# Retention values as seven block products in one stage, retention as one run of 32 chunks, rotation beside the queries' and keys' products

## The chip, the cores and the metric

The kernel runs on one core of a Trainium2 chip. The metric is the device time of one execution in microseconds, as the median of several runs; lower is better. The engines of the core work side by side, each through its own list of instructions in order: TensorE (PE, with its weight loads shown as PEld), VectorE (DVE), ScalarE (ACT), GpSimd (POOL) and SyncE (SP), which here only starts DMA transfers. POOL starts transfers too, through a queue of its own, among them those that add what they carry to what lies at their destination.

## The reference

One decoder block on a sequence of 1024 tokens of width 1024. Its input is normalised and modulated to `h`; `h @ w_in` gives everything that the two mixers need. The part that the change concerns is retention, with 4 heads, keys of 256, values of 512 and chunks of 128 tokens:

```
rq = rotary(heads(rq, RET_HEADS), pos)
rk = rotary(heads(rk, RET_HEADS), pos) * (RET_DK ** -0.5)
ro = retention(rq, rk, heads(rv, RET_HEADS))
...
    def step(state, inp):
        qi, ki, vi = inp
        s = jnp.einsum('bhid,bhjd->bhij', qi, ki) * inner_decay[None]
        o = (jnp.einsum('bhij,bhje->bhie', s, vi)
             + jnp.einsum('bhid,bhde->bhie', qi, state) * q_decay[None, :, :, None])
        state = (state * chunk_decay[None, :, None, None]
                 + jnp.einsum('bhjd,bhje->bhde', ki * k_decay[None, :, :, None], vi))
        return state, o
...
ro = group_norm(ro) * gn_g + gn_b
ret_out = (jax.nn.silu(rg) * ro) @ w_ret_out
```

`rv` is a product of 1024 tokens by 1024 inputs by 2048 columns (512 a head), `rg` the same size. Beside this stand twelve heads of dilated attention, two gates, the output projections and an MLP.

## The kernel before

Every product is done in float32 by three passes: each operand is split into a high part, which PE takes at full rate, and a low part, the rest; `mm3` (line 195) multiplies low by high, high by low and high by high into one PSUM bank. A split is a copy on ACT (high) and a subtraction on DVE (low).

The steps run in this order: input norm and the attention's values (`av_first`, `av_step`); the queries' and keys' stage (`queries_keys`, line 976); then for each of four heads the retention values (`v_first`, `v_rest`) and eight chunks (`chunk`); then attention, projections and MLP. `Steps` holds the list of steps with their weight loads: loads go out on SP's queue into a ring of three tiles (`wraw`, tag `raw`), `prepare` splits them, and a step's body may call `ahead(n)` to have the next step's loads prepared at that point of its own work. `first["release"]` lets the loads of the next group of steps start.

The queries' and keys' stage multiplies in blocks. `h` and the weights are cut into 2 x 2 blocks, and the product of a pair of 128-column tiles is done by seven block products in place of eight (`Blocks`, line 213; `ORDER` names the seven: 11, s1, s3, s2, 12, 22, s4). The sums of blocks of `h` (`t1` to `t4`) are formed once by `sums_of_h`; `t4` takes the place of the second halves of the even tiles `hh`, `hl`, which are saved to memory before (`h12_d`) and brought back at the end of the stage by eight POOL transfers (lines 994 and 995). `BA.run` goes through 18 pairs (`PAIRS`) times seven products; after each it calls `post`, which turns finished banks into outputs, and `before` and `after`, in which loads and the end of the stage are placed by hand. A pair is of retention (`r`), attention (`a`) or gates (`g`), and the string in `PAIRS` gives their order. Outputs and temporaries are tiles of `xpool` (`x4`, a ring of 26). At the start of this stage `weight_sums` has POOL form the seven blocks of the output projection's weights in memory, by `dma_sum`: one transfer writes, a second adds, and each waits for the one whose result it takes.

The retention values are plain products: per head `v_first` does the first half of the depth for the first four chunks, `v_rest` the rest, 8 chunks x 8 depth tiles x 3 matmuls. Between them lie the previous head's last transposition (`on_T`) and its gating (`u_final`: two ACT passes that scale and shift, a DVE multiply by the Silu of `rg`, a write-out to `y_d`), and in `v_rest` the rotation of the head's queries and keys, six DVE operations on 1024 columns for each of the two (`rotate`).

A chunk does on PE, in this order: the new state's terms (`kv`), a half of its share of the gate product `rg`, the next chunk's scores and key transposition (`s_kt`), the chunk's output (`o`, from the state's high and low part and from the scores), the transposition of the previous chunk's normalised output (`on_T`), the rest of `rg`. On DVE: the state's update (line 737), weight preparation (`ahead`), the scores' decay and split, the state's low part, statistics and normalisation (lines 760 to 766). PSUM outside `rg` is a ring of four banks in this part, so `o` takes the bank of the first `kv`.

Of the kernel before, what the change touches and what calls it, by code (L numbers as in the profile page):

```python
# [17 lines left out]
P = 128  # L18
# [116 lines left out]
def block_kernel(ctx, tc, io, stop=None, dbg=None):  # L135
# [191 lines left out]
    xpool = x_ctx.enter_context(tc.tile_pool(name="xpool", bufs=1))  # L327
# [203 lines left out]
    ws_d = {n: dram.tile([P, 4, 1024], F32, name=f"wro{n}") for n in ("11", "12", "22", "s1", "s2", "s3", "s4")}  # L531
# [7 lines left out]
    def weight_sums(t):  # L539

        for i, v in enumerate((VC_GNG, VC_GNB)):
            nc.vector.tensor_copy(gnv[i][:, :16], vec[:, v:v + 16])
            nc.vector.tensor_scalar_mul(gnv[i][:, 16:], vec[:, v:v + 16], -1.0)
        nc.gpsimd.tensor_tensor(pad[:, NK:NK + 1], fv(t)[:, :1], mhalf[:, :1], op=ALU.mult)
        b11, b12, b21, b22 = (io["w_ret_out"][i] for i in range(4))
        dma_sum(ws_d["s1"], b21, b22)
        dma_sum(ws_d["s3"], b21, b11)
        dma_sum(ws_d["s2"], ws_d["s1"], b11)
        dma_sum(ws_d["s4"], ws_d["s2"], b12)
        for n, b in (("11", b11), ("12", b12), ("22", b22)):  # L550
            nc.gpsimd.dma_start(ws_d[n], b)
# [8 lines left out]
    hd = {}  # L560

    def new_head(h):
        hd["qk"] = R["p"].tile([P, 4, S], F32, tag="qk", name=f"qk{h}")
        for i in range(4):
            nc.sync.dma_start(hd["qk"][:, i, :], qk_d[h][i])

    def rotate(h, i):

        x1, x2 = hd["qk"][:, 2 * i, :], hd["qk"][:, 2 * i + 1, :]
        cos, sin = cs[:, 0, :], cs[:, 1, :]  # L570
        t1, t2 = etile(f"t1_{h}{i}"), etile(f"t2_{h}{i}")
        nc.vector.tensor_mul(t2, x2, sin)
        yield
        nc.vector.tensor_mul(t1, x1, sin)
        yield
        nc.vector.tensor_mul(x1, x1, cos)
        yield
        nc.vector.tensor_mul(x2, x2, cos)
        yield
        nc.vector.tensor_sub(x1, x1, t2)  # L580
        yield
        nc.vector.tensor_add(x2, x2, t1)
        yield

    qk_d = [[dram.tile([P, S], F32, name=f"qkd{h}{i}") for i in range(4)] for h in range(H)]
# [4 lines left out]
    def wv_prep(raw):  # L590
        hi, lo = etile(raw.name + "vh", F32R), etile(raw.name + "vl", F32R)
        nc.scalar.copy(hi, raw)
        nc.vector.tensor_sub(lo, raw, fv(hi))
        return hi, lo

    def jit_qk(h, c):
        p = R["p"]
        src = hd["qk"][:, :, c * C:(c + 1) * C]
        t = p.tile([P, 2, 4, C], F32R, tag="j", bufs=2, name=f"j{h}{c}")
        nc.scalar.copy(t[:, 0], src)  # L600
        nc.gpsimd.tensor_sub(t[:, 1], src, fv(t[:, 0]))  # L601
        hd["j", c] = t

    def s_kt(h, c):

        p = R["p"]
        t = hd["j", c]
# [7 lines left out]
        if pk is not None:  # L615
            for i in range(2):
                nc.tensor.transpose(pk[:, i, :], hd["qk"][:, 2 + i, c * C:(c + 1) * C], ident)
# [8 lines left out]
        hd["s", c] = (smh, sml)  # L626
        if pk is not None:
# [5 lines left out]
            hd["k", c] = (kh, kl)  # L633

    def v_mm(ps, wv, c, ks=range(NK)):

        tok = slice(c * C, (c + 1) * C)
        for k in ks:
            w = wv[k // 2]
            ws = slice((k % 2) * 512, (k % 2) * 512 + 512)  # L640
            nc.tensor.matmul(ps, hl[k][:, tok], w[0][:, ws], start=k == 0, stop=False)  # L641
            nc.tensor.matmul(ps, hh[k][:, tok], w[1][:, ws], start=False, stop=False)  # L642
            nc.tensor.matmul(ps, hh[k][:, tok], w[0][:, ws], start=False, stop=k == NK - 1)  # L643

    def v_first(h):

        def body(ahead, *ws):
            hd["wv"] = list(ws)
            mms = [ps_mm(f"v{h}{i}") for i in range(2)]
            pss = hd["vp"] = [mms[c // 2][:, c % 2, :] for c in range(4)]  # L650
            for c in range(4):
                v_mm(pss[c], ws, c, range(4))
                if c == 1 and h > 0:
                    on_T(h - 1, NC - 1)
                    u_final(h - 1, (0, 1))
                    ahead(0)
                    u_final(h - 1, (2, 3))
            ahead(0)
        return body

    def v_rest(h):
        def body(ahead, *ws):
            p = R["p"]
            ws = hd["wv"] + list(ws)
            vh, vl = [], []
            for c in range(0, NC, 2):
                for lst, n in ((vh, "vh"), (vl, "vl")):
                    t = vtile(f"{n}{h}{c}", F32R)
                    lst += [t[:, :DV], t[:, DV:]]
            hd["v"] = list(zip(vh, vl))  # L670
            rot = itertools.chain(rotate(h, 0), rotate(h, 1))
            for n, c in enumerate((0, 2, 1, 3, 4, 5, 6, 7)):
                if c < 4:
# [1679 lines left out]
```

## Time and profile before

| | |
|---|---|
| median of 3 runs | 2267.89 us (2263.89 to 2268.91) |
| the profiled execution's own time | 2273.85 us |
| its span in the profile | 2272.1 us |
| PE busy | 2207.8 us, 97% |
| DVE busy | 1430.8 us, 63% |
| ACT busy | 884.5 us, 39% |
| POOL busy | 119.6 us, 5% |
| DMA | 345.97 MB, mean 152 GB/s |
| mean granted clock of PE | 0.995 |

In the profile, Lnn is a line of the kernel; `out<-in` names tiles without their numbers; an `x` and a number count instructions; the figure in brackets behind a row is the engine's idle time just before it and what ended that. Windows are stretches of the span, in us from its start. A matmul row's duration runs to its modelled end, so rows overlap.

### The profile page before, as it was taken

How to read it: one execution, taken by the hardware profiler on the slowest of the kernel's cores; microseconds unless marked ns; L12 is line 12 of the kernel's file. 1: busy time of each engine (PE TensorE's matmuls, PEld its weight loads, DVE VectorE, ACT ScalarE, POOL GpSimd, SP SyncE). 2: the span in 40 equal slices, each digit the busy share in tenths (PEclk: the TensorE clock that was granted, in tenths of full speed). 3: DMA queues.
4: the chain of work that ended last, by engine and by line, in shares of the span. 5: the costliest groups of instructions: out<-in, count | busy, mean ns of one | idle time of the engine just before them, and what ended most of it. 6: DMA issues, size and time to landing. Idle time of an engine off the chain costs nothing.

```text
span 2272.1 us, 26840 instructions
## 1 busy us (share of the span) xinstructions
PE 2207.8 (97%) x10226; PEld 1822.8 (80%) x10226; DVE 1430.8 (63%) x2201; ACT 884.5 (39%) x1629; POOL 119.6 (5%) x132
## 2 busy tenths in 40 slices
PE   7999999999999999999999999999999999999998
PEld 5887878888878787888878788888777777788887
DVE  6525565546768776764555554576866665787845
ACT  4323233222434333344534633434454444433412
POOL 0000000001102010100000000002100000000003
PEclk9999999999999999999999999999999999999999
DMA  9549933334322323239822345645134443654322
GB/s 357 198 145 259 308 122 109 111 110 148 121 93 84 131 73 139 75 106 268 234 84 89 108 176 205 242 161 175 63 140 146 153 153 138 246 172 167 121 84 75
DMA packets 125903, 345.97 MB, mean 152 GB/s; under 512 B 24358, under 2 KB 35885, under 8 KB 123054
## 3 DMA queue, kind: packets, MB, share of 16 engines
q1 hardware_dynamic: 121726, 302.31, 38.2%
q0 software_dynamic: 4048, 41.94, 6.9%
q8 instruction: 80, 1.31, 0.2%
q14 instruction: 49, 0.40, 0.1%
HBM read 270.13 MB, written 116.28 MB: 170 GB/s over the span
## 4 chain that ended last, share of the span: by engine, by line
PE 73%; DVE 11%; DMA 8%; ACT 5%; issue 2%; SPq 0%; POOL 0%; DVEq 0%; POOLq 0%; ACTq 0%
PE av L799 4%; PE qap L201 3%; PE qap L205 3%; PE qap L203 3%; PE rg L201 3%; PE rg L203 3%; PE rg L205 3%; PE fp L201 2%; PE fp L203 2%; PE fp L205 2%; PE v L641 2%; PE v L643 2%; PE v L642 2%; PE f2a L203 2%; PE f2a L205 2%
## 5 line engine op out<-in xcount | busy, mean ns | idle before, releaser
L201 PE MATMUL qap<-hh,qaw 128*128 128x512 f32 x216 | 85.2, 395 | 6.8 <-ACT qat L280 4.8
L203 PE MATMUL qap<-hl,qaw 128*128 128x512 f32 x216 | 84.5, 391 | 0.0
L205 PE MATMUL qap<-hh,qaw 128*128 128x512 f32 x216 | 84.5, 391 | 0.0
L258 DVE TENSOR_TENSOR qaw<-wa,qaw 128x512 fp32r<-128x512 f32 x54 | 36.6, 690 | 50.9 <-ACT qaw L248 50.5
L1817 ACT ACTIVATE a<-a 128x512 f32<-128x512 f32 x48 | 30.3, 632 | 84.8 <-DVE a L1816 84.8
L601 POOL TENSOR_TENSOR j<-qk,j 128x512 fp32r<-128x512 f32 x32 | 43.9, 1370 | 366.0 <-ACT j L600 366.0
L1170 ACT ACTIVATE P<-P,ng 128x128 f32<-128x128 f32 (+1 forms) x96 | 41.9, 438 | 39.2 <-DVE ng L1167 39.2
L258 DVE TENSOR_TENSOR fw<-w1r,fw 128x512 fp32r<-128x512 f32 x48 | 33.0, 688 | 37.5 <-ACT fw L248 37.5
L201 PEld LDWEIGHTS qap<-hh,qaw 128*128 128x128 f32 x216 | 40.9, 189 | 16.9 <-ACT qat L280 5.6
L2001 ACT CAST w2h<-w2s 128x512 fp32r<-128x512 f32 x36 | 22.4, 621 | 79.9 <-DVE w2s L2039 79.9
L679 ACT CAST vh<-v 128x512 fp32r<-128x512 f32 x32 | 18.8, 587 | 88.1 <-PE v L643 86.0
L621 ACT COPY sm<-sT 128x128 f32<-128x128 f32 x32 | 8.5, 266 | 114.1 <-PE sT L612 114.1
L248 ACT CAST qaw<-wa 128x512 fp32r<-128x512 f32 x54 | 32.4, 617 | 46.8 <-PE qap L205 28.0
L201 PE MATMUL fp<-h2h,fw 128*128 128x512 f32 x128 | 50.0, 390 | 0.0
L203 PE MATMUL fp<-h2l,fw 128*128 128x512 f32 x128 | 49.8, 389 | 0.0
L201 PE MATMUL roa<-rh,rwl 128*128 128x512 f32 x128 | 49.8, 389 | 0.0
L203 PE MATMUL roa<-rl,rwh 128*128 128x512 f32 x128 | 49.8, 389 | 0.0
L205 PE MATMUL roa<-rh,rwh 128*128 128x512 f32 x128 | 49.8, 389 | 0.0
L205 PE MATMUL fp<-h2h,fw 128*128 128x512 f32 x128 | 49.8, 389 | 0.0
L1714 POOL TENSOR_TENSOR accnf<-accnf,sqnf 128x256 f32<-128x256 f32 (+1 forms) x18 | 16.6, 921 | 628.1 <-ACT sqnf L1713 628.1
L1551 DVE TENSOR_TENSOR rwl<-rwl,rwh 128x1024 fp32r<-128x1024 f32 x25 | 30.2, 1221 | 29.0 <-ACT rwh L1582 29.0
L203 PEld LDWEIGHTS qap<-hl,qaw 128*128 128x128 f32 x216 | 41.0, 190 | 8.5
(3161 smaller groups left out, 7162.2 us busy)
## 6 DMA issues: line engine op xcount, KB each, us to landing
raw<-in_w_ada_dram SPq DMA_DIRECT2D x32, 512.0 KB, 3.5
w1r<-in_w_ff_dram SPq DMA_DIRECT2D x32, 512.0 KB, 4.9
yt<-y POOLq DMA_DIRECT2D x6, 2048.0 KB, 16.2
xsd<-as SPq DMA_DIRECT2D x24, 512.0 KB, 2.7
w2r<-in_w_ff2s_dram SPq DMA_DIRECT2D x24, 512.0 KB, 7.2
em<-in_w_ada_dram SPq DMA_DIRECT2D x16, 512.0 KB, 10.2
wros<-in_w_ret_out_dram POOLq DMA_DIRECT2D x4, 2048.0 KB, 16.4
qkd<-qa SPq DMA_DIRECT2D x16, 512.0 KB, 3.0
```

The lines of the kernel that those rows point to most:

```text
L201: nc.tensor.matmul(o, wl, xh, start=first, stop=False, skip_group_check=skip)
L203: nc.tensor.matmul(o, wh, xl, start=False, stop=False, skip_group_check=skip)
L205: nc.tensor.matmul(o, wh, xh, start=False, stop=last, skip_group_check=skip)
L248: nc.scalar.copy(t[:, :512], src)
L258: nc.vector.tensor_sub(t[:, 512:], src, fv(t[:, :512]))
L601: nc.gpsimd.tensor_sub(t[:, 1], src, fv(t[:, 0]))
L641: nc.tensor.matmul(ps, hl[k][:, tok], w[0][:, ws], start=k == 0, stop=False)
L642: nc.tensor.matmul(ps, hh[k][:, tok], w[1][:, ws], start=False, stop=False)
L643: nc.tensor.matmul(ps, hh[k][:, tok], w[0][:, ws], start=False, stop=k == NK - 1)
L799: nc.tensor.matmul(av[g][c], x[k][:, c * C:(c + 1) * C], w[j][:, ws], start=k == 0 and (x, j) == parts[0], stop=k == NK - 1 and (x, j) == ...
L1170: nc.scalar.activation(v, v, AF.Exp, bias=ng[:, blk:blk + 1], accum_out=st[:, g, blk, 2 + a:3 + a])
L1817: nc.scalar.activation(o, o, AF.Relu)
```

## The change

The values are formed for all heads in one stage behind the queries' and keys' products, by seven block products for each of two halves of the columns: 14 items (`VSEQ`), each four token tiles. The weights' blocks come from memory, summed by POOL at the start of the queries' and keys' stage, ahead of the output projection's. The items take the sums of `h` as the stationary operand; results leave already split, as high and low part, for `v_d`. The restores of `hh` and `hl` and the release of the next loads move behind the first token tile of the last item. `fetch` then brings, three chunks ahead, a chunk's rotated queries and keys (256 KB) and its values (512 KB).

The rotation is taken into the queries' and keys' stage: after each product one DVE operation on 512 columns for the retention pair before, 12 a pair, and then the write-out to `qk_d`. `PAIRS` is reordered so that retention pairs are spread out. `xpool` gets the option `reuse_waits="tile"`, which the other pools of the later stages have already.

The 32 chunks follow each other without a values' stage between them. The gating of a head is done one tile at a time at the end of the first four chunks of the next. In the first chunk of all, its whole share of `rg` goes ahead of `kv`. `u_final`, `on_T`, `s_kt` and `jit_qk` keep their instructions, indexed by a running number. The code leaves out `v_first`, `v_rest`, `new_head`, `wv_prep`, `vtile` and the old `rotate`.

```diff
-    xpool = x_ctx.enter_context(tc.tile_pool(name="xpool", bufs=1))
+    xpool = x_ctx.enter_context(tc.tile_pool(name="xpool", bufs=1, reuse_waits="tile"))
...
-        return R["p"].tile([P, 1024], dt, tag="E", bufs=8, name=name)
-
-    def vtile(name, dt=F32):
-        return R["p"].tile([P, 1024], dt, tag="V", bufs=8, name=name)
+        return R["p"].tile([P, 1024], dt, tag="E", bufs=12, name=name)
...
+        for dst, src in ((wv_d, io["w_rv"]), (ws_d, io["w_ret_out"])):
+            b11, b12, b21, b22 = (src[i] for i in range(4))
+            dma_sum(dst["s1"], b21, b22)
+            dma_sum(dst["s3"], b21, b11)
+            dma_sum(dst["s2"], dst["s1"], b11)
+            dma_sum(dst["s4"], dst["s2"], b12)
+            for n, b in (("11", b11), ("12", b12), ("22", b22)):
+                nc.gpsimd.dma_start(dst[n], b)
...
+    def fetch(i):
+
+        h, c = divmod(i, NC)
+        if i > 1:
+            hd["qk", i] = R["p"].tile([P, 4, C], F32, tag="qk", bufs=4, name=f"qk{h}{c}")
+        elif i == 0:
+            t = whl.tile([P, 1024], F32, tag="wl", name="qk01").rearrange("p (a b c) -> p a b c", a=2, b=4)
+            for j in range(2):
+                hd["qk", j] = t[:, j]
+                nc.sync.dma_start(t[:, j], qk_d[0][:, :, j * C:(j + 1) * C])
+        if i > 1:
+            nc.sync.dma_start(hd["qk", i], qk_d[h][:, :, c * C:(c + 1) * C])
+        if i > 0:
+            v = R["p"].tile([P, 2, DV], F32R, tag="V", bufs=4, name=f"v{h}{c}")
+        else:
+            v = whl.tile([P, 1024], F32R, tag="wh", name="v00").rearrange("p (a b) -> p a b", a=2)
+        hd["v", i] = v
+        nc.sync.dma_start(fv(v), v_d[h][:, c])
...
     def chunk(h, c, ahead, w=None):
         p = R["p"]
-        if c == 0:
-            hd["srg"] = [etile(f"srg{h}{e}") for e in range(4)]
+        g = NC * h + c
+        if g + 3 < NG:
+            fetch(g + 3)
         if c % 2 == 0:
             hd["rgw"] = w
             hd["rgp"] = ps_mm(f"rg{h}{c}")
-        if c == 6 and h + 1 < H:
-            new_head(h + 1)
         ks = range(4 * (c % 2), 4 * (c % 2) + 4)
-        vh, vl = hd["v"][c]
+        if g == 0:
+            proj_mm(hd["rgp"], hd["rgw"], ks)
...
-            on_T(h, c - 1)
-        proj_mm(hd["rgp"], hd["rgw"], ks[2:])
+        if g + 2 < NG:
+            jit_qk(g + 2)
+        if g > 0:
+            on_T(*divmod(g - 1, NC))
+        if g > 0:
+            proj_mm(hd["rgp"], hd["rgw"], ks[2:])
...
-        hd["o", c] = on
+        hd["o", h, c] = on
         if c % 2 == 1:
-            nc.scalar.activation(hd["srg"][c // 2], flat(hd["rgp"]), AF.Silu)
-
-    def head_tail(h):
-        on_T(h, NC - 1)
-        u_final(h)
+            hd["srg", h, c // 2] = etile(f"srg{h}{c // 2}")
+            nc.scalar.activation(hd["srg", h, c // 2], flat(hd["rgp"]), AF.Silu)
+        if h > 0 and c < 4:
+            u_final(h - 1, (c,))
...
-    PAIRS = [{"r": r_pairs, "a": a_pairs, "g": g_pairs}[i].pop(0) for i in "ragragragragrrarar"]
+    PAIRS = [{"r": r_pairs, "a": a_pairs, "g": g_pairs}[i].pop(0) for i in "rargrargrargrargaa"]
...
+    def rotate(q):
+
+        _, t, h = PAIRS[q]
+        u, v = BA.t[q]
+        for hf in range(2):
+            hs = slice(512 * hf, 512 * hf + 512)
+            x1, x2, cos, sin = OA[q][0][:, hs], OA[q][1][:, hs], cs[:, 0, hs], cs[:, 1, hs]
+            for f, o, x, y in ((nc.vector.tensor_mul, u, x2, sin), (nc.vector.tensor_mul, v, x1, sin),
+                               (nc.vector.tensor_mul, x1, x1, cos), (nc.vector.tensor_mul, x2, x2, cos),
+                               (nc.vector.tensor_sub, x1, x1, u), (nc.vector.tensor_add, x2, x2, v)):
+                f(o, x, y)
+                yield
+        for i in range(2):
+            nc.sync.dma_start(qk_d[h][:, 2 * (t == "k") + i], OA[q][i])
...
+        turns = []
         def after(q, n):
-            if q == NA - 1 and n == "s2":
-                first["release"]()
+            if turns:
+                next(turns[0], None) or None
+            if n == ORDER[-1] and PAIRS[q][0] == "r":
+                while turns:
+                    drain(turns.pop())
+                turns.append(rotate(q))
+            if q == NA - 1 and n in ("12", "s4"):
+                v_load(n == "s4")
             if q == NA - 1 and n == "22":
-                for m in range(4):
-                    nc.gpsimd.dma_start(hh[2 * m][:, 512:], h12_d[m][:, 0])
-                    nc.gpsimd.dma_start(hl[2 * m][:, 512:], h12_d[m][:, 1])
-                ahead(2)
+                for j in range(2):
+                    v_w(0, j)
 
         BA.run([(q, n) for q in range(NA) for n in ORDER], sums, before, after)
+        while turns:
+            drain(turns.pop())
+        values(ahead)
+    VPLAN = {"11": ("11", 1, "a"), "12": ("21", 1, "b"), "s1": ("t1", 1, "c"), "s2": ("t2", -1, "a"),
+             "s3": ("t3", -1, "a"), "22": ("t4", -1, "a"), "s4": ("22", 1, "c")}
+    VSEQ = [(hp, n) for hp in range(2) for n in VPLAN]
...
+    def v_load(i):
+
+        hp, n = VSEQ[i]
+        for j in range(2):
+            lo = V["w", i, j] = v_place(i, "l", j)
+            nc.sync.dma_start(fv(lo), wv_d[n][:, 2 * hp + j])
+
+    def v_w(i, j):
+        lo, hi, sign = V["w", i, j], v_place(i, "h", j), float(VPLAN[VSEQ[i][1]][1])
+        nc.scalar.activation(hi, fv(lo), AF.Copy, scale=sign)
+        V["w", i, j] = hi, lo
+        V["low", i, j] = lo, hi, sign
+
+    def v_low(i, j):
+        lo, hi, sign = V.pop(("low", i, j))
+        if sign > 0:
+            nc.vector.tensor_sub(lo, fv(lo), fv(hi))
+        else:
+            nc.vector.scalar_tensor_tensor(lo, fv(lo), -1.0, fv(hi), op0=ALU.mult, op1=ALU.subtract)
+
+    def v_mm(i, p):
+        hp, n = VSEQ[i]
+        x, _, bank = VPLAN[n]
+        new = n in ("11", "12", "s1")
+        if new:
+            V["ps", bank, p] = ps_s(f"v{bank}{hp}{p}")
+        for m in range(4):
+            xh, xl = (t[:, p * P:p * P + P] for t in XA[x, m])
+            wh, wl = (t[:, 512 * (m % 2):512 * (m % 2) + 512] for t in V["w", i, m // 2])
+            mm3([V["ps", bank, p]], (xh, xl), [(wh, wl)], new and m == 0, m == 3, True)
+
...
+        if n != "s4":
+            t = wraw.tile([P, 2, DV], F32R, tag="raw", name=f"vo{i}{p}")
+        if n == "22":
+            nc.scalar.mul(t[:, 0], ps, -1.0)
+            nc.vector.scalar_tensor_tensor(t[:, 1], ps, -1.0, fv(t[:, 0]), op0=ALU.mult, op1=ALU.subtract)
+        else:
+            src, dst = {"12": (r1, r1), "s3": (r2, r2), "s4": (r1, r2)}[n]
+            (nc.vector.tensor_sub if n == "s3" else nc.vector.tensor_add)(dst, src, ps)
+            nc.scalar.copy(t[:, 0], dst)
+            nc.vector.tensor_sub(t[:, 1], dst, fv(t[:, 0]))
+        blk = {"12": "11", "s4": "12", "s3": "22", "22": "21"}[n]
+        nc.sync.dma_start(v_d[2 * hp + int(blk[0]) - 1][:, p + 4 * (int(blk[1]) - 1)], fv(t))
+    def values(ahead):
+        last = len(VSEQ) - 1
+        for j in range(2):
+            v_low(0, j)
+        for i, (hp, n) in enumerate(VSEQ):
+            if i + 2 <= last:
+                v_load(i + 2)
+            for p in range(4):
+                v_mm(i, p)
+                if V["post"]:
+                    v_post(*V["post"].pop())
+                V["post"].append((i, p))
+                if p < 2 and i < last:
+                    v_w(i + 1, p)
+                    if p:
+                        v_low(i + 1, 0)
+                if p == 2 and i < last:
+                    v_low(i + 1, 1)
+                if i == last - 1 and p == 3:
+                    fetch(0)
+                if i == last and p == 0:
+                    for m in range(4):
+                        nc.gpsimd.dma_start(hh[2 * m][:, 512:], h12_d[m][:, 0])
+                        nc.gpsimd.dma_start(hl[2 * m][:, 512:], h12_d[m][:, 1])
+                    first["release"]()
+                if i == last and p == 1:
+                    jit_qk(0)
+                    jit_qk(1)
+                if i == last and p == 2:
+                    ahead(2)
+        v_post(*V["post"].pop())
+        open_ret()
+        for g in (1, 2):
+            fetch(g)
+        s_kt(0)
         banks(False)
-        open_ret()
-        new_head(0)
 
```

More of the change, by code (lines that the diff above doesn't have):

```diff
@@ L529, in block_kernel @@
     YB = ("11", "12", "21", "22")
-    ws_d = {n: dram.tile([P, 4, 1024], F32, name=f"wro{n}") for n in ("11", "12", "22", "s1", "s2", "s3", "s4")}
+    WN = ("11", "12", "22", "s1", "s2", "s3", "s4")
+    wv_d = {n: dram.tile([P, 4, 1024], F32, name=f"wrv{n}") for n in WN}
+    ws_d = {n: dram.tile([P, 4, 1024], F32, name=f"wro{n}") for n in WN}
     def dma_sum(out, x, y):
@@ L645, in v_first @@
[L645 to L673, printed above, removed]
[L674 to L690 removed]
+            hd["k", g] = (kh, kl)
@@ L998, in queries_keys, with v_place @@
         BA.run([(q, n) for q in range(NA) for n in ORDER], sums, before, after)
+        while turns:
[4 more added lines that the diff above has]
+    VSEQ = [(hp, n) for hp in range(2) for n in VPLAN]
+    V = {"post": []}
+    def v_place(i, part, j):
+        name = f"vw{part}{i}{j}"
+        return whl.tile([P, 1024], F32R, tag="w" + part, name=name) if i % 3 == 1 and i < 13 else x4(name, F32R)
@@ L1014, in block_kernel @@
     for h in range(H):
-        steps.add(v_first(h), [wsplit(io["w_rv"][4 * h + j]) for j in range(2)], manual=True)
-        steps.add(v_rest(h), [(io["w_rv"][4 * h + j], wv_prep) for j in range(2, 4)], manual=True)
         for c in range(NC):
```

132 lines of the change are left out of this document (49 added, 83 removed).

## The prediction

> **What bounds the kernel.** I read the page's engine table first, then busy time by stage, then what ended the idle time of TensorE (PE) and of the queues, then the order of time at the places that the change touches.
>
> ```profile
> span 2272.1 us, 26840 instructions
> PE 2207.8 (97%) x10226; PEld 1822.8 (80%) x10226; DVE 1430.8 (63%) x2201; ACT 884.5 (39%) x1629; POOL 119.6 (5%) x132
> ```
>
> PE is busy for 97% of the span. An operation on another engine costs time only where it makes PE wait; a matmul less is a matmul's time won. What such a time is, the order of time shows at the seam between the queries' and keys' stage and the first head's values:
>
> ```profile
> 511.73 0.39 PE L205 MATMUL qap<-hh,qaw17s 128*128 128x512 f32 x1
> 511.95 0.39 PE L641 MATMUL v<-raw_3529h,hl 128*128 128x512 f32 x1
> ...
> 515.81 0.39 PE L643 MATMUL v<-raw_3529h,hh 128*128 128x512 f32 x1
> ```
>
> Columns: start, duration, engine, line, operation. One matmul is listed with 0.39 us, but they overlap: from 511.95 to 515.81 lie 18 rows, 17 steps, so 0.227 us from start to start. That, and not 0.39, is the price of a 512-column product here. Next, the stages: columns are the window, its length, busy time of PE, PEld, DVE, ACT and POOL with counts, the granted clock, the busy share of the DMA engines and GB/s.
>
> ```profile
> 182.00:512.00 330.00, 326.93 (x1435) 269.90 (x1434) 177.77 (x262) 95.65 (x161) 9.09 (x16) 0.99 0.52 170
> 555.00:636.00 81.00, 81.00 (x392) 67.53 (x391) 58.18 (x122) 32.13 (x79) 12.53 (x14) 1.00 0.32 104
> 636.00:679.00 43.00, 41.00 (x183) 33.01 (x182) 30.13 (x33) 15.45 (x27) 2.79 (x2) 1.00 0.29 98
> 760.00:803.00 43.00, 41.00 (x184) 32.98 (x182) 30.09 (x33) 15.46 (x27) 2.79 (x2) 1.00 0.29 98
> 883.00:927.00 44.00, 42.01 (x188) 33.82 (x187) 30.12 (x33) 15.46 (x27) 2.79 (x2) 1.00 0.30 96
> ```
>
> The first row is the queries' and keys' stage, the second one head's eight chunks, the last three the values of heads 1 to 3. The chunks leave PE no gap; each of the three value stages loses 2.0 us.
>
> **Matmuls removed.** Before, a head's values are 8 chunks x 8 k x 3 = 192 matmuls, 768 in all. After, there are 14 block products of 4 token tiles x 4 k-tiles x 3 = 48, so 672. 96 fewer at 0.227 us is **-21.8 us**. The Trainium skill (TensorE: Matmul & The Clock Gate, "Back-to-back issue gap") gives N/2.4 + 2.5 ns, 216 ns for 512 columns; by that page it would be an estimated -20.7 us. The rows above show 0.227, and the rows decide.
>
> **Stalls removed.** The three 2.0 us gaps come from the head boundary, where the weights' high halves wait for a tile whose write-out has not landed:
>
> ```profile
> ACT raw_4585vh L592 <- DMA y<-on: 1.8, 1, 1.8
> PE v L642 <- DVE raw_4585vl L593: 1.3, 1, 1.3
> ```
>
> With one run of chunks, a new head allocates no such weights at that point, and its result tiles come from a ring of 12 in place of 8. I take all of it: 3 x 2.0 = **-6.0 us**.
>
> **Weight sums, doubled.** The same 11 POOL transfers of 2 MB that form the output projection's blocks now run first for the values' blocks. The old run stands here, with what it did to PE:
>
> ```profile
> 166.58 0.72 POOL L536 DMA_DIRECT2D wros<-in_w_ret_out_dram  x1
> 247.85 1.81 POOL L551 DMA_DIRECT2D wro<-in_w_ret_out_dram  x3
> 247.04 8.58 DMA wa<-in_w_rq_dram
> 263.76 21.99 DMA wa<-in_w_aq_dram
> 260.00:280.00 20.00, 20.00 (x90) 16.56 (x89) 9.59 (x14) 5.24 (x9) 0.00 (x0) 1.00 1.05 364
> 280.00:300.00 20.00, 16.93 (x67) 13.25 (x66) 10.29 (x17) 6.83 (x12) 0.00 (x0) 0.91 0.49 181
> 300.00:320.00 20.00, 20.00 (x90) 16.55 (x89) 12.22 (x18) 5.12 (x9) 0.00 (x0) 1.00 0.30 106
> 285.82 0.62 ACT L248 CAST qaw<-wa 128x512 fp32r<-128x512 f32 x1 [11.45 <-DMA wa<-in_w_aq_dram]
> 292.13 0.79 PE L201 MATMUL qap<-hh,qaw 128*128 128x512 f32 x1 [2.73 <-ACT qat L280]
> 292.73 0.63 PE L203 MATMUL qap<-hl,qaw 128*128 128x512 f32 x1
> ```
>
> The sums run from 166.6 to about 285 us and fill the DMA engines (share 1.05). At their end three 2 MB copies are in flight at once, a weight load takes 21.99 us, ACT stands still for 11.45 us behind it, and PE gets 67 matmuls into 20 us where its neighbours get 90: 23 x 0.227 = 5.2 us lost. The loss is more than the 2.73 us of waiting because the matmuls behind it start 0.6 us apart (292.13, 292.73) and the clock of that window is 0.91. The Trainium skill (TensorE: Matmul & The Clock Gate, "What's actually happening") says that PE falls to half its clock after an idle window of about 3.4 us; here 2.73 us of idle were followed by the slow stretch, so by the trace the margin is smaller. After the change two such batches run one behind the other, to about 400 us by the first's length, still before the values' stage at about 512. I take one more stall of this size, **+5.2 us**; from 0, if the loads happen to fall between the copies, to 20, if three or four more loads meet the copies.
>
> **Rotation moved.** It leaves the values' stages, where its 48 operations took 1.22 us each, and becomes 96 of half the width beside the block products, one after each product:
>
> ```profile
> L572 DVE TENSOR_TENSOR t<-qk,cossin x8: 1214/1216/1218, 527.0 to 906.1; 128x1024 f32<-128x1024 f32 x8
> L258 DVE TENSOR_TENSOR qaw<-wa,qaw 128x512 fp32r<-128x512 f32 x54 | 36.6, 690 | 50.9 <-ACT qaw L248 50.5
> ```
>
> 96 x 0.69 = 66 us on DVE, which has 177.8 of 330 us there: 74% afterwards. A product takes 12 x 0.227 = 2.7 us, and DVE's mean work per product becomes 177.8/126 + 0.69 = 2.1 us; the operands are prepared several products ahead, so PE covers it: 0. Its two write-outs per pair move two pairs later on SP's queue, and the tiles stay held as long. If that cover goes, it goes together with the sums (rival 1).
>
> **Seam before the values.** The new stage's first weights are split on DVE behind the last post of the old one, so PE waits for that chain:
>
> ```profile
> 510.04 1.22 DVE L192 TENSOR_TENSOR raw_3529l<-raw,raw_3529h 128x1024 fp32r<-128x1024 f32 x1
> 512.31 0.68 DVE L962 TENSOR_TENSOR qa<-qat,qap 128x512 f32<-128x512 f32 x1
> ```
>
> The post can start at 512.31, the low half is there 0.68 + 1.22 later, 514.2; the second matmul, the first to need it, could have begun at 512.18. **+2.0 us** (0 if the order on DVE turns out otherwise, 3.7 if half a slow stretch follows).
>
> **The values' stage itself.** An item is 48 x 0.227 = 10.9 us. DVE has at most two 1.22 us splits and eight 0.69 us posts, 8.0 us. Per item 1 MB is read and in four of seven 2 MB written: 3.1 MB in 10.9 us is 289 GB/s, below the 364 of the row 260 to 280, and weights are loaded two items ahead. 0, up to 6 if the write-outs hold up the posts.
>
> **Seam before the chunks.** During the last item the 2 MB of activations come back (eight POOL issues), the first chunk's tiles and gate weights are loaded, and the last values written: about 6.5 MB in 10.9 us, more than the rows so far moved. The old seam had the same restores:
>
> ```profile
> 507.89 0.58 POOL L994 DMA_DIRECT2D hh<-h12d  x1 [258.23 <-ACT qa L960]
> 511.90 0.53 POOL L995 DMA_DIRECT2D hl<-h12d  x1
> 515.00:520.00 5.00, 5.00 (x24) 4.14 (x23) 0.00 (x0) 0.20 (x1) 0.00 (x0) 1.00 1.10 339
> DMA to landing us min/median/max: 3.1/6.6/10.5
> 508.14 1.05 ACT L191 CAST raw_3531h<-raw 128x1024 fp32r<-128x1024 f32 x1
> ```
>
> Then, 24 matmuls of values on unrestored tokens covered them; now the first chunk begins with gate products that read both halves and need their weights split (1.05 us on ACT, 1.22 on DVE). The weight load can go out some 2.5 us into the item, lands 6.6 to 10.5 us later, is split by 11.4 to 15.3; PE arrives at about 12. From 0 to 12; I take **+3.0 us**, near the upper landing. The wait for the weights stands on ACT ahead of the copies of the last values, which free the banks that the chunk needs. A first head's value tiles queue on SP behind these, a chunk ahead of need.
>
> **The chunks.** One head's gating (two ACT passes and a multiply for each of four tiles) moves from the values' stage into the first four chunks of the next head, behind the gate's Silu in odd ones. DVE is nearly full there:
>
> ```profile
> 604.90 0.81 DVE L766 TENSOR_SCALAR onm<-o,ba,gr 128x512 f32<-128x512 f32 x1
> 605.64 1.37 DVE L737 SCALAR_TENSOR_TENSOR state<-state,kv 128x512 f32<-128x512 f32 x2
> 614.91 0.81 DVE L766 TENSOR_SCALAR onm<-o,ba,gr 128x512 f32<-128x512 f32 x1
> 642.28 1.22 DVE L710 TENSOR_TENSOR on<-on,srg 128x1024 f32<-128x1024 f32 x1 [0.18 <-ACT on L708]
> L769 ACT ACTIVATE srg<-rg x16: 1027/1029/1029, 575.9 to 1003.8; 128x1024 f32<-128x1024 f32 x16
> L708 ACT ACTIVATE on<-on,gnt x32: 797/817/846, 639.3 to 1015.3; 128x512 f32<-128x512 f32 x32
> 564.74 0.39 PE L201 MATMUL kv<-vh,kl 128*128 128x512 f32 x1
> 569.38 0.48 PE L201 MATMUL o<-stateh,j 128*128 128x512 f32 x1
> ```
>
> A chunk is 10.0 us (604.90 to 614.91), DVE's list is as long in an odd chunk, and 1.22 us is added, behind Silu (1.03 us) and two passes of 0.82 us on ACT. The state's update then starts some 2.6 us late after chunk 1 and 3.6 after chunk 3; even chunks give back about 1.4. What waits is the next output product, which takes the update's PSUM bank: it begins 4.6 us after the chunk's first matmul, and the update is normally done at about 1.6 (605.64 and half of 1.37, less 604.75, four chunks behind 564.74), so 3.0 us are free. 0.5 us lost once a head, in three heads: **+1.5 us** (0 to 9, three times that free time).
>
> **The sum.** -21.8 - 6.0 + 5.2 + 2.0 + 3.0 + 1.5 = -16.1 us. The profiled execution took 2273.85 us, 1.75 more than its span and 6.0 more than the median of 2267.89, so it would become 2257.8. I take the difference over to the median: 2251.8, say **2252**. With every cost at its lower end it is -27.8, 2240.
>
> **Rivals.** *1, slower: the sums starve the queries' and keys' stage.* Two batches hold the DMA engines full for some 240 us, 13 pairs of 19 us. Loads took 8.6 to 22 us then, about as long as a pair; the rotated tiles are now held two pairs longer in the same ring of 26, so a late write-out also blocks new tiles. For: ACT's 11.45 us and the single stall. Against: before that stall, PE shows no gap from 182 to 280 though the DMA share is near 1. It decides from 2.0 us lost per pair over 13 pairs (26 us against what is left of the gain); at 3 us it gives 39, in place of 5.2: -16.1 - 5.2 + 39 = +17.7, 2286. The Trainium skill (DMA: Bandwidth & Descriptors, "Anatomy of one DMA", arbitration) says that a DMA engine goes round its queues packet by packet; by that rule POOL's copies take turns with SP's loads through both batches, and the load of 21.99 us agrees.
>
> *2, no change: DVE becomes the bound of the chunks with gating.* Then each of 12 such chunks costs the 1.22 us it adds, 14.6 in place of 1.5: -3.0, 2265. For: DVE's odd chunk without a real gap. Against: the 1.4 us that even chunks have free.
>
> *3, faster still: the loads and restores fall into place.* Only the seam before the values remains: -25.8, 2242.
>
> That it does not do what it says could only be if PE's products were not 672; the diff's loops leave no room for it.
>
> **How the numbers follow.** Forecast 0.68, rival 1 0.14, rival 2 0.10, rival 3 0.08. A measurement can tell 0.2%, 4.5 us, from no change. Rival 3 and most of the forecast are faster, 0.72; rival 1 and a part of rival 2 with a longer seam slower, 0.18; the rest, 0.10, the same. Range: 2240, with all costs hidden, to 2274, which takes in rival 2 and a seam of 12 us, and leaves out rival 1's larger losses.
>
> **What would show it.** 672 value matmuls 0.227 us apart, in one stage of about 152 us; no gap at the three head boundaries; DMA share near 1 until about 400 us with two short gaps of PE, each with a dip of the clock; a gap of 2 us before the values and a few us before the first gate products; chunk windows with PE at its full time. I am wrong if PE's idle time in 182 to 512 exceeds some 15 us, if the output products of chunks wait for DVE in most chunks, or if the seam before the chunks is over 10 us.

## The result: slower by half a per cent

The changed kernel takes 2279.01 us (median of 6 runs, 2276.30 to 2288.53); beside them the kernel before takes 2268.40. The ratio is 1.0054, 95% interval 1.0033 to 1.0075. The prediction was 2252, with a range of 2240 to 2274: the sign was wrong, and the range missed it. The profiled execution of the changed kernel took 2277.95 us.

The page of the changed kernel begins so:

```profile
span 2276.1 us, 27081 instructions
PE 2189.8 (96%) x10130; PEld 1808.0 (79%) x10130; DVE 1454.4 (64%) x2285; ACT 908.5 (40%) x1665; POOL 126.0 (6%) x143
```

PE has exactly 96 matmuls less (10226 to 10130) and 18 us less of busy time, yet the span grew. So the products were saved, and more than they were worth went into waiting. The waits of PE between 150 and 760 us, longest first (total, times, longest):

```profile
PE rg L201 <- DVE kl L628: 13.6, 1, 13.6
PE qap L201 <- DVE qat L285: 10.7, 5, 5.9
PE qap L201 <- ACT qat L280: 9.2, 2, 6.9
PE kv L201 <- DVE kl L628: 2.5, 1, 2.5
PE va L203 <- DVE vwlFalse L995: 2.1, 1, 2.1
```

There are two places: the queries' and keys' stage (qap, 19.9 us, where the kernel before has 6.8) and the seam between values and chunks (rg and kv, 16.1 us). By window, columns as in the prediction, first the changed kernel:

```profile
182.00:280.00 98.00, 98.00 (x434) 81.14 (x433) 68.04 (x107) 28.59 (x48) 5.71 (x9) 1.00 0.97 296
280.00:420.00 140.00, 122.84 (x515) 99.60 (x514) 90.62 (x141) 36.93 (x64) 6.59 (x10) 0.94 0.84 264
700.00:703.00 3.00, 2.99 (x7) 2.41 (x8) 0.00 (x0) 0.00 (x0) 0.00 (x0) 0.50 0.94 289
740.00:1000.00 260.00, 260.00 (x1268) 216.20 (x1267) 209.55 (x437) 124.04 (x311) 51.12 (x54) 1.00 0.56 182
```

and the second of these windows in the kernel before:

```profile
280.00:420.00 140.00, 136.93 (x597) 112.60 (x596) 80.03 (x120) 43.43 (x75) 0.00 (x0) 0.99 0.34 124
```

Between 280 and 420 us PE gets 515 matmuls done where it did 597: 82 x 0.227 = 18.6 us late. (Three variants below leave this stage as it is; their values begin at 529.1, 531.5 and 535.9 us where the changed kernel's begin at 530.5, so this loss differs by some us between executions.) The same number comes out of where the stages begin. The products of the values (va) and of attention's keys (ak), by tile, in the changed kernel (columns: shortest, median and longest ns, first and last start in us):

```profile
L201 PE MATMUL va<-vwh,hl x64: 388/389/389, 530.5 to 673.7; 128*128 128x512 f32 x64
L201 PE MATMUL ak<-hh,raw_7723l x16: 389/389/481, 1014.8 to 1025.1; 128*128 128x512 f32 x16
```

and ak in the kernel before, whose first value product stands in the prediction at 511.95:

```profile
L201 PE MATMUL ak<-hh,raw_7548l x16: 389/389/481, 1003.6 to 1013.8; 128*128 128x512 f32 x16
```

From the first value to the last chunk it takes 1014.8 - 530.5 = 484.3 us in place of 1003.6 - 511.95 = 491.6: 7.4 gained. Up to there 18.6 were lost. 18.6 - 7.4 = +11.2, and the medians differ by 10.6. (The rest, from ak to the end of the span, was 1268.5 us before and 1261.3 after; six variants below that leave it as it is have 1261.7 to 1266.4, so this part differs by some us between executions.)

**What happens at the seam.** The changed kernel in order of time, on SP's queue, then ACT, then DVE, then PE:

```profile
676.88 0.70 SPq L85 DMA_DIRECT2D raw<-in_w_rg_dram  x1
683.46 0.62 ACT L594 CAST j<-qk 128x512 fp32r<-128x512 f32 x1 [4.85 <-DMA qk<-qkd]
686.89 0.62 ACT L594 CAST j<-qk 128x512 fp32r<-128x512 f32 x1 [2.81 <-DMA qk<-qkd]
690.62 1.04 ACT L191 CAST raw_4649h<-raw 128x1024 fp32r<-128x1024 f32 x1 [2.60 <-DMA raw<-in_w_rg_dram]
692.84 1.22 DVE L450 SCALAR_TENSOR_TENSOR raw<-raw,cb 128x1024 f32<-128x1024 f32 x1
696.15 0.68 DVE L1032 TENSOR_TENSOR vr<-vr,vc 128x512 f32<-128x512 f32 x1
699.47 0.48 DVE L628 SCALAR_TENSOR_TENSOR kl<-kT,ct,kh 128x256 fp32r<-128x256 f32 x1
700.01 1.22 PE L201 MATMUL rg<-hh,raw_4649l 128*128 128x512 f32 x2 [13.59 <-DVE kl L628]
```

ACT stands three times for a load: the queries of the first chunk, those of the second, the gate's weights. Behind these stand the last values' results (vr), behind them the first chunk's scores and keys (kl), and the gate product (rg) waits for kl because the banks are divided anew after the scores are issued. It is one chain through three queues. The gate's weights alone were split by 692.9, 7.1 us earlier. This wait repeats well: the four variants below that leave the seam as it is (the rotation left out and the three edits of the sums) have 13.0 to 14.3 us.

### The profile page after: what moved, and what is told of

Same layout as the page of the kernel before. It is cut to its first block, busy times and chain, and to the rows that moved or that the text cites. A ratio compares the mean times of both kernels' runs of the same rounds, so it can differ in the third digit from the quotient of the medians.

```text
span 2276.1 us, 27081 instructions
## 1 busy us (share of the span) xinstructions
PE 2189.8 (96%) x10130; PEld 1808.0 (79%) x10130; DVE 1454.4 (64%) x2285; ACT 908.5 (40%) x1665; POOL 126.0 (6%) x143
## 4 chain that ended last, share of the span: by engine, by line
PE 75%; DVE 11%; DMA 5%; ACT 5%; issue 2%; SPq 0%; POOL 0%; POOLq 0%; DVEq 0%; ACTq 0%
PE av L742 4%; PE qap L201 3%; PE qap L205 3%; PE qap L203 3%; PE rg L201 3%; PE rg L203 3%; PE rg L205 3%; PE fp L201 2%; PE fp L203 2%; PE fp L205 2%; DMA wa<-in_w_rq_dram 2%; PE ak L201 2%; PE f2a L203 2%; PE f2a L205 2%; PE f2a L201 2%
## 5 line engine op out<-in xcount | busy, mean ns | idle before, releaser
L201 PE MATMUL qap<-hh,qaw 128*128 128x512 f32 x216 | 87.7, 406 | 19.9 <-DVE qat L285 10.7
L201 PEld LDWEIGHTS qap<-hh,qaw 128*128 128x128 f32 x216 | 42.0, 194 | 31.8 <-DVE qat L285 13.1
L205 PEld LDWEIGHTS qap<-hh,qaw 128*128 128x128 f32 x216 | 42.0, 194 | 9.1
## 6 DMA issues: line engine op xcount, KB each, us to landing
yt<-y POOLq DMA_DIRECT2D x6, 2048.0 KB, 15.3
```

The source lines that it names most:

```text
L201: nc.tensor.matmul(o, wl, xh, start=first, stop=False, skip_group_check=skip)
L205: nc.tensor.matmul(o, wh, xh, start=False, stop=last, skip_group_check=skip)
```

## Experiments

Two questions were put: is the first stage's loss due to the two batches of sums or to the rotation, and is the seam's wait due to late loads or to the order of work? Ratios are against the kernel before, run on the same chip; the changed kernel stands at 1.0054.

**The rotation left out.**

```diff
-                turns.append(rotate(q))
+                pass
 ...
```

(and the unrotated halves are written at once)

> The changed kernel without the rotation: queries and keys are written out unrotated, at once, so that neither DVE's 96 operations nor the longer held tiles are there. Batch theory: the stalls stay, first value at 527 to 531, 2276 to 2279 us. Rotation theory: first value at about 512 to 515, 2261 us.

Measured: 2277.51 us, 1.0037 (1.0025 to 1.0050).

```profile
PE qap L201 <- ACT qat L280: 15.3, 4, 7.2
PE qap L201 <- DVE qat L285: 3.4, 3, 1.7
L201 PE MATMUL va<-vwh,hl x64: 388/389/628, 529.1 to 673.8; 128*128 128x512 f32 x64
```

The first two rows are PE's waits, the last the values' products by tile. 18.7 us of waits stay, and the values begin 1.4 us earlier. In this kernel the rotation costs at most that; the rest isn't its doing.

**One batch beside the queries and keys**, the output projection's sums put behind the result's sums in attention.

```diff
-        for dst, src in ((wv_d, io["w_rv"]), (ws_d, io["w_ret_out"])):
+        block_sums(wv_d, io["w_rv"])
 ...
                 result_sums()
+                block_sums(ws_d, io["w_ret_out"])
```

> The changed kernel, with the output projection's weight sums moved behind the result sums in the attention stage; the queries' and keys' stage has one batch of 11 POOL transfers, for the values. That stage ended 18.6 us later than before. Batch theory (each batch of sums stalls PE): the stall at 289 to 296 stays, the ones at 320 to 409 (10 us of waiting, and some 3 us of half clock) go: first value at about 518 in place of 530.5, 2268 us if attention does not pay for the moved batch. Rotation theory (rotation's DVE work and its longer held tiles stall PE): first value still at about 530, 2279.

Measured: 2282.60 us, 1.0070 (1.0044 to 1.0095). The values by tile (PE's longest wait in attention is now 10.9 us):

```profile
L201 PE MATMUL va<-vwh,hl x64: 388/389/628, 513.2 to 657.9; 128*128 128x512 f32 x64
```

The window 1075 to 1400, in this kernel and in the changed one:

```profile
1075.00:1400.00 325.00, 298.51 (x1557) 252.43 (x1557) 167.10 (x263) 135.77 (x285) 8.84 (x13) 0.96 0.68 206
```

```profile
1075.00:1400.00 325.00, 314.91 (x1686) 266.99 (x1685) 176.56 (x275) 148.19 (x316) 2.84 (x3) 1.00 0.49 154
```

The values begin 17.3 us earlier: the second batch costs most of what the first stage lost. But moved as one burst into attention it stalls that stage by about as much: 16.4 us less PE time in 325 us. (This profiled execution took 2290.67 us, 8 more than the median.)

**The same, with the values' sums released one at a time**, by a one-column operation on POOL that reads a temporary of a pair, and so waits for that pair's first product.

```diff
+            if n == "11":
+                nc.gpsimd.tensor_tensor(pad[:, NK:NK + 1], BA.t[q][0][:, :1], mhalf[:, :1], op=ALU.mult)
+                next(pace, None)
 ...
```

> As the run before, and the values' sums are paced: one of the 11 transfers per pair, by a one-column POOL operation on a temporary of that pair. Batch theory: never more than one 2 MB copy in flight, no stall of PE in the queries' and keys' stage, first value at about 511, 2261 us. Rotation theory: first value at about 530, 2279.

Measured: 2274.03 us, 1.0033 (1.0013 to 1.0053). The values begin at 506.7 us, and PE has no wait over 2.1 us from 150 to 530 us. Against the 513.2 of the run before, one batch with its burst costs 6.5 us. The output projection's burst is still paid in attention:

```profile
PE pt010(0, 0, 0)_9064 L1370 <- DVE P L1353: 8.4, 1, 8.4
```

**Both batches where the change put them, each of 22 transfers released alone**: 18 beside the pairs, four beside items of the values' stage.

```diff
+    def pace(t):
+        nc.gpsimd.tensor_tensor(pad[:, NK:NK + 1], t[:, :1], mhalf[:, :1], op=ALU.mult)
+        while paces and next(paces[0], 1):
+            paces.pop(0)
 ...
+            if n == "11":
+                pace(BA.t[q][0])
 ...
+            if i in (1, 3, 5, 7):
+                pace(fv(V["w", i, 0][0]))
 ...
```

> Both batches of weight sums stay in the stages where the change put them, but one transfer is released at a time by a one-column GpSimd operation: 18 beside the 18 pairs of queries and keys, the last four beside four items of the values' stage. Crowding theory (22 transfers queued at once slow the loads of the same stage, and spread out they have room): the first product of the values starts at about 507 us as in the kernel with paced values' sums (506.7) instead of 530.6, no stage later pays, and the time is 2276 - 24 = about 2253 us, faster than before. Bytes theory (the second 30 MB or so of traffic cannot fit in any stage before attention without delaying loads): some stage pays them back, the first value late by 10 us or the chunks late by as much, and the time stays at 2265 us or more.

Measured: 2256.13 us (2255.25 to 2258.59), 0.9939 (0.9923 to 0.9956). The window, and the products by tile:

```profile
280.00:420.00 140.00, 140.00 (x619) 115.95 (x619) 105.40 (x165) 43.02 (x75) 8.99 (x16) 1.00 0.69 229
```

```profile
L201 PE MATMUL va<-vwh,hl x64: 388/389/628, 507.4 to 652.1; 128*128 128x512 f32 x64
L201 PE MATMUL ak<-hh,raw_7745l x16: 389/389/481, 992.5 to 1002.8; 128*128 128x512 f32 x16
```

The same sums, the same number of transfers, and PE is full from 280 to 420. The values begin 23.1 us earlier than in the changed kernel and hardly anything is given back: ak comes 22.3 us earlier. A group of weight loads between 182 and 420 (size, median us to landing), here and in the changed kernel; the other three groups have 4.5 to 5.4 here and 9.3 to 16.1 there:

```profile
wa<-in_w_gate_dram SPq DMA_DIRECT2D x7, 512.0 KB, 4.5
```

```profile
wa<-in_w_gate_dram SPq DMA_DIRECT2D x4, 512.0 KB, 19.6
```

And what lies behind it, in the changed kernel: from its chain of work one of these loads (start, duration), then POOL in order of time, then ACT.

```profile
257.24 30.84 DMA wa<-in_w_gate_dram
```

```profile
243.47 1.82 POOL L551 DMA_DIRECT2D wrv<-in_w_rv_dram  x3
244.94 0.83 POOL L535 DMA_DIRECT2D wros<-in_w_ret_out_dram  x1
287.00 0.91 POOL L536 DMA_DIRECT2D wros<-in_w_ret_out_dram  x1 [41.23 <-DMA wros<-in_w_ret_out_dram]
```

```profile
288.10 0.62 ACT L248 CAST qaw<-wa 128x512 fp32r<-128x512 f32 x1 [12.71 <-DMA wa<-in_w_gate_dram]
295.76 0.58 ACT L280 COPY qat<-qap 128x512 f32<-128x512 f32 x1
```

Here is the burst: at the end of the first batch three plain copies are issued with nothing between them, and the second batch's first copy right behind. These four transfers of 2 MB go out within 2 us, 0.6 us behind an add of the same size (242.88), the last of them lands at about 287, and a 512 KB load issued among them takes 30.84 us. ACT stands 12.71 us for it, and the copy that frees a bank for PE, the one named in the first stall of 6.9 us, stands behind that on ACT, until 295.76. A full DMA share alone isn't it: from 182 to 280, at 0.97, PE lost nothing. Paced, the same bytes cost PE nothing here: their bunching is what the changed kernel pays for. Pacing lowers both the number of transfers in flight and the mean share (0.69 in place of 0.84 from 280 to 420), and which of the two counts more wasn't separated.

**The banks divided anew before the first scores.**

```diff
-        s_kt(0)
         banks(False)
+        s_kt(0)
```

> The changed kernel with one edit: the PSUM banks are divided anew before the first chunk's scores and key transposition instead of behind them. In the changed kernel the first gate product waits 13.6 us, until 700.0, for the key's low half, which is read from a bank that it is to take; the gate weights' low half is ready at 692.9 already. Order theory (the wait is for banks and for work in front on ACT and DVE): the gate product starts at about 693, 7 us earlier, near 2272 us. Transfer theory (only the late weights and restored tiles count): under 1 us, 2279.

Measured: 2276.24 us, 1.0038 (1.0023 to 1.0053).

```profile
697.06 1.22 PE L201 MATMUL rg<-hh,raw_4649l 128*128 128x512 f32 x2 [10.08 <-DVE vr L1032]
```

Half of what order theory expected: the wait falls by 3.5 us, and then the next link holds, the values' last results. (The intervals of the time, in this run and the two that follow, overlap that of the changed kernel or just touch it; the waits tell more.)

**The last results ahead of the weights' split, with the banks first.**

```diff
-                if i == last and p == 2:
-                    ahead(2)
         v_post(*V["post"].pop())
+        ahead(2)
 ...
```

> The changed kernel with the banks divided anew ahead of the first chunk's scores, as in the run with the banks first, and the split of the first gate weight and the preparation of the next modulation put behind the values' last results. Order theory: the gating product no longer waits for the values' last sums, which that run showed at 697.1 us; it starts when the weight is split, 690.6 us landed + 1.0 + 1.2 = about 693 us, and the wait is about 6 us; the time is 2276 - 4 - 4 = some 2270 us. Transfer theory: the wait stays at 9 us or more, since the last results stand behind the copies of queries and keys that wait for their own transfer (683 and 687 us).

Measured: 2275.93 us, 1.0030 (1.0016 to 1.0043); the wait is 8.3 us, now for the weights:

```profile
697.35 1.04 ACT L191 CAST raw_4649h<-raw 128x1024 fp32r<-128x1024 f32 x1
699.70 1.22 PE L201 MATMUL rg<-hh,raw_4649l 128*128 128x512 f32 x2 [8.33 <-DVE raw_4649l L192]
```

Neither theory's number: the split now stands behind the results, and both behind the copies of the queries. (All of this stage lies some 5 us later in this execution than in the changed kernel's.)

**Two loads earlier.**

```diff
-                if i == last - 1 and p == 3:
-                    fetch(0)
+                if i == last - 2 and p == 1:
+                    fetch(0)
+                if i == last - 1 and p == 3:
+                    first["issue"](RG0 + 1)
 ...
```

> The changed kernel with two loads of the seam issued earlier: the first chunk's queries, keys and values two items of the values' stage (some 24 us) earlier, the first gate weight one block (2.7 us) earlier and now ahead of everything else on its queue. Transfer theory of the seam (the wait of 13.6 us before the chunks is the loads' lateness, which holds up ScalarE and VectorE and with them the last values' results): the wait falls to about 4 us, and the time by about 10 us to 2268 us. Order theory (the wait is set by the order of the banks and of the last values' results on ScalarE and VectorE): the wait falls by less than 4 us, the time by no more than that.

Measured: 2274.24 us, 1.0022 (1.0011 to 1.0033); the wait is 7.65 us in place of 13.59.

```profile
685.07 1.23 DVE L451 SCALAR_TENSOR_TENSOR raw<-raw,cb 128x1024 f32<-128x1024 f32 x1 [2.96 <-DMA raw<-in_w_ada_dram]
692.24 1.22 PE L201 MATMUL rg<-hh,raw_4625l 128*128 128x512 f32 x2 [7.65 <-DVE kl L629]
```

Between the two theories. The next load in line, the modulation's, now holds DVE for 2.96 us ahead of the last results. So it is both: each late load matters because work that doesn't need it stands behind it.

**All together**: both batches paced, loads early, banks first, only the weight's split (not the modulation) ahead of the last results, and the first chunk's gate product in two parts like the others'.

> Paced sums, early loads, banks first, the modulation's preparation behind the values' last results, and the first chunk's gating product in two parts like that of the other chunks, so that its second part covers the 2.5 us wait for the next chunk's keys. If crowding and the seam are the two causes and add up: first value at 507 us, wait before the chunks about 3 us, no second wait; against the changed kernel -24 - 10 - 2.5 - about 2 of half clock, together some 2238 us, 30 us faster than before. If the gains are given back later (attention waits longer for what the chunks leave it), 2250 us or more.

Measured: 2244.18 us (2241.72 to 2246.02), 0.9884 (0.9864 to 0.9904): 25 us faster than the kernel before on that chip, 12 faster than with pacing alone. The products by tile, and PE at the seam in order of time:

```profile
L201 PE MATMUL va<-vwh,hl x64: 388/389/395, 506.3 to 649.4; 128*128 128x512 f32 x64
L201 PE MATMUL ak<-hh,raw_7745l x16: 389/389/481, 977.7 to 987.9; 128*128 128x512 f32 x16
```

```profile
661.98 0.74 PE L201 MATMUL rg<-hh,raw_4647l 128*128 128x512 f32 x2 [0.21 <-DVE vr L1045]
668.88 0.80 PE L201 MATMUL kv<-v,kl 128*128 128x512 f32 x1 [3.89 <-DVE kl L640]
```

The gate product waits 0.2 us. One wait of 3.9 us is left, for the first chunk's keys, with the clock at half behind it (last section). From the first value to ak it takes 471.4 us, 12.9 less than in the changed kernel, where 14.5 were expected. The expected 2238 starts from the changed kernel's span of 2276.1; this span is 2242.5, and of the 5 us between, 1.6 lie at the seam and 3.5 behind ak (1264.8 us against 1261.3), in the part that differs between executions. Which of the four edits at the seam is worth how much in this combination wasn't separated.

## Why the prediction was wrong

*Right.* 96 matmuls at 0.227 us, -21.8: the count is in the page of the profile, and from va to ak the last version takes 977.7 - 506.3 = 471.4 us, 20.2 less than before, with 4.1 us of waits left at its seam. Head boundaries, -6.0, the values' stage at 0 and the gating in the chunks (+1.5, of which nothing shows): PE is busy for 260.00 of 260 us from 740 to 1000, across the three boundaries. The seam before the values, +2.0: 2.1, by the chain that the prediction named. The rotation at 0: 1.4 at most.

*The first step that failed: the size of the sums' term, +5.2 us.* Place and mechanism were right (DMA share near 1 to 400 us, two short stretches with gaps of PE, each with a dip of the clock), and the condition given for being wrong, over 15 us of idle in 182 to 512, came true: 17.2. The size was 18.6. The prediction took one more stall as large as the old one. There are two stretches, one a batch, but each costs more than twice the old stall. The changed kernel by slices:

```profile
280.00:300.00 20.00, 13.07 (x51) 10.34 (x50) 9.14 (x14) 4.00 (x7) 1.42 (x2) 0.84 0.92 248
300.00:320.00 20.00, 18.41 (x80) 14.93 (x79) 13.38 (x22) 5.13 (x9) 1.39 (x2) 0.99 1.03 349
380.00:400.00 20.00, 14.06 (x55) 11.31 (x55) 7.67 (x13) 2.98 (x5) 0.00 (x0) 0.83 0.87 311
400.00:420.00 20.00, 17.84 (x72) 14.26 (x71) 16.13 (x27) 7.97 (x14) 0.00 (x0) 0.91 0.20 79
```

A full slice has 90 products. From 280 to 320 there are 49 too few (and 3 more up to 340), together 11.8 us, and from 380 to 420 there are 53 too few, 12.0 us; less the old 5.2 that is 18.6. The first stretch follows the first batch's burst, with eleven more transfers behind it; with one batch alone it was 6.5 us. The second follows the three plain copies of the second batch, issued at 360.58 us with nothing behind them. There ACT stands, by the trace, for write-outs of attention's queries that have not landed, and PE's wait of 5.94 us ends at 386.16:

```profile
383.45 0.62 ACT L248 CAST qaw<-wa 128x512 fp32r<-128x512 f32 x1 [8.76 <-DMA aqd<-qa]
394.45 0.62 ACT L248 CAST qaw11s<-qas 128x512 fp32r<-128x512 f32 x1 [10.38 <-DMA aqd<-qa]
```

That is rival 1's late write-out, which blocks new tiles. From 182 to 512 us ACT stands 21.3 us for write-outs and 17.6 for loads; without the rotation and its longer held tiles it is 2.6 and 49.3, and the values begin only 1.4 us earlier. So the held tiles change what is waited for, not the loss. Why this stretch lost 12 us where the old batch lost 5.2 stays open. The row that would have warned is the load of 21.99 us quoted in the prediction, where another in the same batch took 8.58: it says what a load beside such a burst costs. The bound of 20 held; the value was taken near the wrong end. Rival 1 had this mechanism, at 3 us a pair over 13 pairs; by the runs it was about half of its price, enough with the seam for its sign. (The rule on taking turns that rival 1 quotes from the Trainium skill, DMA: Bandwidth & Descriptors, stands there under "Queues, rings and completion order"; the long loads agree with it but don't show it.)

*The second step: the seam before the chunks, +3.0 us, at most 12.* The sign given for it, over 10 us, came true as well. It is 13.6 + 2.5, and some 2 us for the half clock behind these two waits (484.3 us less 491.6 is -7.4; -21.8 - 6.0 + 2.1 + 13.6 + 2.5 is -9.6). The prediction followed one load, the gate's weights, to its split and compared that with PE's arrival: 11.4 to 15.3 us into the item, against 12. On that path the load itself was later than the latest landing it allowed: out at 676.88, landed at 690.62, 13.7 us in place of 6.6 to 10.5. The split was done at 692.9, 6.5 us after PE had come to the end of its work (686.4), and that alone is twice the +3.0. But the product began only 7.1 us after that. What the prediction left out was that three loads, the modulation's preparation, the last results and the first chunk's keys share ACT's and DVE's queues, so that their lateness adds up, and that rg waits for all of it through the banks. The prediction had the clue in a half-sentence (the weights' wait "stands on ACT ahead of the copies of the last values, which free the banks that the chunk needs") and didn't price it.

*The range.* 2274 is rival 2's 2265 with the seam at 12; it never took the sums at 20 together with the seam at 12. Both costs are of one kind, loads late at a DMA share near 1, though they are two events: with the sums paced the seam's wait is still 13.0 and 13.5 us. Both at their upper ends give -16.1 + 14.8 + 9 = +7.7, or 2276, still 3 us short of the measured time. Rival 2's cost, which made the range reach 2274, did not appear.

## What to carry to other kernels

Background transfers are paid by how they are bunched: release them one at a time by something that the foreground produces, and the same bytes may cost nothing, as in the run with 22 paced transfers. At a seam, list all that stands on each queue between the last old and the first new product, not only what the new product reads; a wait for a load in that list holds everything behind it. When an edit moves the wait only to the next link, make the edits together before judging any of them.

## What the hardware showed

A 512 KB load issued among four 2 MB transfers between places of the chip's memory took 30.84 us, against a median of 4.5 us in one group with such transfers one at a time. Whether this is shared throughput alone, or also the order in which the queues are served, these runs don't separate.

PE's clock can fall to half behind a wait of 2 to 2.5 us, and need not. The wait before the values is 2.07 us in the changed kernel and in all eight variants. In the 4 us behind it the clock was 1.00 in the changed kernel and four variants, and 0.57 to 0.59 in the other four (one batch, values' sums paced, no rotation, both batches paced). Behind the wait of 2.52 us at the seam it was 0.60 to 0.64 in five kernels and 1.00 in three (no rotation, early loads, last results first). Behind every wait of 3.5 us or more between 150 and 1060 us, 13.59 among them (row 700 to 703 above), it fell. The changed kernel behind its 2.07 us, the run with one batch around its own 2.07, and the last version behind 3.89:

```profile
533.00:537.00 4.00, 4.00 (x18) 3.31 (x19) 1.08 (x1) 0.00 (x0) 0.00 (x0) 1.00 0.99 307
512.00:531.00 19.00, 16.93 (x68) 13.50 (x68) 5.86 (x6) 5.32 (x7) 0.00 (x0) 0.91 0.62 222
670.00:674.00 4.00, 4.00 (x14) 3.41 (x13) 2.96 (x7) 0.27 (x1) 0.00 (x0) 0.50 1.05 399
```

The Trainium skill (TensorE: Matmul & The Clock Gate, Part 1) lets the clock fall after an idle window of about 3.4 us; here shorter waits were enough in some executions and not in others, and what decides it these runs don't show. In the second row 68 products stand where 19 us hold 84: 16 x 0.227 = 3.6 us, so the half clock cost some 1.6 us on top of the wait.
